# Sliding-window attention in a one-core layer kernel: transposing the probabilities in 32 by 32 blocks on VectorE and placing them by on-chip DMAs

## The chip, the cores and the metric

The kernel runs on one core of a Trainium2 chip. A core has engines that work at the same time, each through its own queue, in order: TensorE (PE, with its weight loads PEld), VectorE (DVE), ScalarE (ACT), GpSimd (POOL), and SyncE (SP), which here issues most DMAs; 16 DMA engines move the data. The metric is the device time of one execution in microseconds, lower being better.

## What is computed

One layer on x of 2048 tokens by 1024: token mixing, cross-attention to 256 memory tokens, and a SwiGLU feed-forward, each between RMS norms. Token mixing projects the normed x to 2816 columns: 512 for the queries of a sliding attention (8 heads of 64), 128 for its keys and 128 for its values (2 heads of 64, each for four query heads), and four times 512 for a gated recurrence (HGRN2). The change is in the sliding attention alone:

```python
def swa_with_sinks(q, k, v, sinks):
    # a token of chunk c (64 tokens) reads every token of chunks c-2 .. c
    s = jnp.einsum('bnqhgd,bnkhd->bnhgqk', qc, kband) * (Dh ** -0.5)
    s = jnp.where(valid, s, NEG_INF)
    p = jax.nn.softmax(jnp.concatenate([s, sink], axis=-1), axis=-1)[..., :L]
    return jnp.einsum('bnhgqk,bnkhd->bnqhgd', p, vband)
```

## The kernel before

All is computed in float32 precision. The matmuls of projections and sliding attention run on float32r operands, and an operand is split into a high part (a rounded copy) and a low part (the rest), so that a product is two or three matmuls (`mm3`, L151: high x high, high x low, low x high).

The program has stages. First `in_first` (L466) norms x and projects the first 1024 tokens, writing the columns to `z_d` in device memory, and then key and value columns of the second 1024 tokens. From about 264 to 605 us three things are traced side by side in `mix` (L216 to L237): sliding attention, one position n of 128 tokens at a time (16 of them); the first eight positions of the recurrence; and `in_proj`, which projects the second 1024 tokens, one block of 128 columns at a time, 48 matmuls of 512 columns each (L156 to L158). Then the rest of the recurrence with the folding of the cross-attention's weights, and from about 760 us the output projection, cross-attention and feed-forward as large products (L1162 to L1164).

The program is written as generators that take turns, but what stands in each engine's queue is decided by a scheduler, which orders the instructions by its own timeline. Once built, each queue is fixed and runs in order, and an instruction that waits holds all behind it on its engine.

A position of sliding attention is in two halves. `swa_front` (L773) loads queries and keys twice, once to partitions 0 to 63 and once to 64 to 127, and splits them on the way: the queries by ScalarE and VectorE (L787, L788), the keys by GpSimd and VectorE (L798). Because high and low parts of the queries stand on the two halves of the partitions, two matmuls do for the scores (L822, L823). VectorE takes mask and maximum (L827), ScalarE the exponentials with their sums (L831), GpSimd and VectorE finish the sink and the reciprocal (L834 to L839), and VectorE scales (L842). `swa_back` (L845) is called one position later. TensorE transposes the probabilities, four blocks of 128 by 128 into one PSUM bank (L856); ScalarE writes their high part (L860), VectorE the low part (L861); TensorE multiplies with the values (L865, L866), whose high and low parts are beside each other, so that the result comes as two halves on the partitions, which are added (L869, L870) and stored to `y_d`. The tiles of this pool have one buffer where no number is given: `kr`, `kl`, `kh`, `ys`; `S` has six, which is three per pair of heads of two positions.

Of the kernel before, what the change touches and what calls it, by code (L numbers as in the profile page):

```python
# [48 lines left out]
class Layer:  # L49
# [111 lines left out]
    def run(self):  # L161
# [4 lines left out]
        self.z_d = tc.dram_tile([DIN, T], F32, name="z_d")  # L166

# [298 lines left out]
    def in_first(self):  # L466
# [154 lines left out]
        z = self.pair_tile()  # L621
        for s in range(2):
            for i in range(2):
# [3 lines left out]
                nc.scalar.activation(z[:, i, s * 512:(s + 1) * 512], ps, AF.Copy)  # L627
        for i in range(2):
            self.store(self.z_d[c0 + i * P:c0 + (i + 1) * P, TB:2 * TB], z[:, i, :])
        return u  # L630

    def in_block(self, ca, cb, x, ahead, beside, get, plain, between):
# [16 lines left out]
        def out(i, j, a, b):  # L649
            c0 = (ca, cb)[i] * P  # L650
            if plain:
                self._n += 1
                t = self.st_pool.tile([P, 512], F32, tag="part", name=f"zp_{self._n}", bufs=3)
                nc.scalar.activation(t, a, AF.Copy)
                self.store(self.z_d[c0:c0 + P, j * 512:(j + 1) * 512], t)
                return
            if not z:
                z.append(self.pair_tile())
            zs = z[0][:, i, j * 512:(j + 1) * 512]
# [16 lines left out]
        def after():  # L676
# [14 lines left out]
            for i, c in enumerate(() if plain else (ca, cb)):  # L691
# [17 lines left out]
    def in_cols(self, b, u, cols, e1):  # L709
# [5 lines left out]
        for s in range(TB // 512):  # L715
            sl = slice(s * 512, (s + 1) * 512)
            for i, c in enumerate(cols):
# [4 lines left out]
                if c0 < C_QH or C_IH <= c0 < C_GH:  # L722
# [11 lines left out]
        for i, c in enumerate(cols):  # L734
# [5 lines left out]
            self.store(self.z_d[c0:c0 + P, b * TB:(b + 1) * TB], z[i])  # L740
# [32 lines left out]
    def swa_front(self, n, kinds):  # L773
# [7 lines left out]
        for g in range(2):  # L781
            qd = ph.tile([P, 4, P], F32, tag="qd", name=f"qd{n}_{g}", bufs=2)
            qsrc = z[g * 256:(g + 1) * 256, t0:t0 + P].rearrange("(h d) t -> d h t", d=64)
            self.load(qd[0:64], qsrc)
            self.load(qd[64:128], qsrc)
            q = ph.tile([P, 4, P], F32R, tag="qs", name=f"qs{n}_{g}", bufs=2)
            nc.scalar.activation(q, qd, AF.Copy, scale=-0.125)  # L787
            nc.vector.scalar_tensor_tensor(q[64:128], qd[64:128], -0.125, f32(q[64:128]), ALU.mult, ALU.subtract)  # L788
            qs.append(q)

        kr = ph.tile([P, 2, M], F32, tag="kr", name=f"kr{n}")
        kl = ph.tile([P, 2, M], F32R, tag="kl", name=f"kl{n}")
        kh = ph.tile([P, 2, M], F32R, tag="kh", name=f"kh{n}")
# [1033 lines left out]
```

## Time and profile before

| | us |
|---|---|
| median of three runs (2533.18, 2534.37, 2536.8) | 2534.37 |
| span of the profiled execution, first to last instruction | 2530.8 |
| stage of sliding attention (264 to 605): VectorE on 62 low parts (L861) | 42.3 |
| the same: ScalarE on 62 high parts (L860) | 36.8 |

The profile is of one execution on the chip, and of it the span is given. A row of a group of instructions gives line, engine, operation, what is written and read, shapes and count, then busy time in us, mean duration in ns, and the engine's idle time before them with what ended it. A row by windows gives for each engine the busy time and the count, then the granted TensorE clock (1.00 is full), the share of the DMA engines, and GB/s. A row of the timeline begins with start and duration. TensorE's matmuls overlap, so one's duration is longer than the time it takes from the queue.

### The profile page before, as it was taken

Reading aid. Unit: us, or ns where it says so; the run is one execution under the profiler, and the core shown is the slowest. Engines: PE = TensorE matmul, PEld = TensorE weight load, DVE = VectorE, ACT = ScalarE, POOL = GpSimd, SP = SyncE. Lnnn points to the kernel's source line nnn. Section 1 sums busy time; section 2 is a strip of 40 time slices with the busy share of each in tenths; the row PEclk is TensorE's granted clock in tenths of the full one; section 3 lists DMA queues with packets and bytes.
Section 4 is the critical chain, followed back from the end, with each engine's and each line's share of the span. In section 5 each row is a group of like instructions: output and inputs, shape, how many; then the busy total and the mean of one; then the engine's idle time right before and its main releaser. Section 6 shows DMA issues by size and latency. Waiting matters only on the chain.

```text
span 2530.8 us, 34134 instructions
## 1 busy us (share of the span) xinstructions
PE 2496.8 (99%) x11942; PEld 2087.0 (82%) x11942; DVE 1794.5 (71%) x2863; ACT 1262.1 (50%) x2627; POOL 375.2 (15%) x540
## 2 busy tenths in 40 slices
PE   9999999999999999999999999999999999999998
PEld 8878888888987888878878888888888888888886
DVE  8785488986557889988866655576566557664766
ACT  5453466655565576566753333353333335443543
POOL 4231344321401111112200000000000000000022
PEclk9999999999999999999999999999999999999999
DMA  6455645673887996758944322254354334565776
GB/s 199 152 167 177 176 145 156 199 248 114 276 311 261 299 335 196 251 175 256 346 161 168 135 77 93 80 192 154 129 208 167 117 130 155 182 178 112 228 173 153
DMA packets 305133, 470.07 MB, mean 186 GB/s; under 512 B 21440, under 2 KB 193472, under 8 KB 304960
## 3 DMA queue, kind: packets, MB, share of 16 engines
q1 hardware_dynamic: 298912, 445.86, 52.7%
q0 software_dynamic: 6048, 22.02, 5.1%
q8 instruction: 94, 1.54, 0.3%
q14 instruction: 79, 0.65, 0.1%
HBM read 301.09 MB, written 166.72 MB: 185 GB/s over the span
## 4 chain that ended last, share of the span: by engine, by line
PE 84%; DVE 6%; DMA 4%; ACT 3%; issue 2%; POOL 1%; SPq 0%; DVEq 0%; POOLq 0%; ACTq 0%
PE psm L1164 23%; PE psm L1162 23%; PE psm L1163 22%; PE psg L156 2%; PE psg L158 2%; PE psg L157 2%; DVE T L1002 1%; DVE S L1002 1%; DMA raw<-in_wo_x_dram 1%; ACT junk L1533 1%; SPq L75 0%; DMA row<-h_d 0%; PE pss L156 0%; PE pss L157 0%; PE pss L158 0%
## 5 line engine op out<-in xcount | busy, mean ns | idle before, releaser
L1162 PE MATMUL psm<-T,S 128*128 128x512 f32 x2680 | 1034.3, 391 | 10.3 <-ACT part L1177 5.6
L1163 PE MATMUL psm<-T,S 128*128 128x512 f32 x2680 | 1042.9, 390 | 1.5 <-DVE T L1002 1.4
L1164 PE MATMUL psm<-T,S 128*128 128x512 f32 x2680 | 1029.8, 390 | 3.7 <-DVE S L1002 3.7
L1162 PEld LDWEIGHTS psm<-T,S 128*128 128x128 f32 x2680 | 503.2, 188 | 122.5 <-ACT part L1177 9.9
L1164 PEld LDWEIGHTS psm<-T,S 128*128 128x128 f32 x2680 | 503.4, 188 | 111.1 <-DVE S L1002 6.7
L1163 PEld LDWEIGHTS psm<-T,S 128*128 128x128 f32 x2680 | 503.5, 188 | 107.2 <-DVE T L1002 3.7
L999 ACT ACTIVATE S<-sum 128x512 fp32r<-128x512 f32 (+1 forms) x370 | 224.3, 620 | 375.7 <-PE psm L1164 274.2
L1002 DVE TENSOR_TENSOR S<-sraw,S 128x512 fp32r<-128x512 f32 (+1 forms) x315 | 212.1, 680 | 237.2 <-ACT S L999 234.1
L1177 ACT ACTIVATE part<-psm 128x512 f32<-128x512 f32 x285 | 168.8, 597 | 260.4 <-PE psm L1164 241.9
L1002 DVE TENSOR_TENSOR S<-sum,S 128x512 fp32r<-128x512 f32 (+1 forms) x388 | 258.5, 675 | 45.2 <-ACT S L999 41.2
L999 ACT ACTIVATE S<-sraw 128x512 fp32r<-128x512 f32 (+1 forms) x300 | 184.4, 618 | 109.2 <-PE psm L1164 107.3
L1566 POOL DMA_DIRECT2D y_d<-row x16 | 14.1, 879 | 1077.0 <-DVE row L1748 1026.1
L1002 DVE TENSOR_TENSOR T<-row,T 128x1024 fp32r<-128x1024 f32 (+1 forms) x112 | 131.0, 1186 | 27.7 <-ACT T L999 25.7
L156 PE MATMUL psg<-u,whi 128*128 128x512 f32 x320 | 127.6, 399 | 1.3 <-DVE z L730 1.3
L158 PE MATMUL psg<-u,wlo 128*128 128x512 f32 x320 | 127.4, 399 | 0.0
L157 PE MATMUL psg<-u,whi 128*128 128x512 f32 x320 | 127.4, 398 | 0.0
L1533 ACT ACTIVATE junk<-row 128x512 f32<-128x512 f32 x160 | 99.7, 625 | 43.5 <-DVE row L1555 21.2
L999 ACT ACTIVATE T<-row 128x1024 fp32r<-128x1024 f32 (+1 forms) x112 | 113.4, 1032 | 7.3 <-DMA row<-in_w_down_dram 2.8
L1699 DVE TENSOR_TENSOR row<-psm,part 128x512 f32<-128x512 f32 x66 | 44.1, 688 | 71.3 <-PE psm L1164 71.3
L1002 DVE TENSOR_TENSOR wlo<-raw,whi 128x1024 fp32r<-128x1024 f32 x52 | 64.0, 1232 | 41.4 <-ACT whi L999 30.6
L1748 DVE TENSOR_TENSOR row<-psm,part 128x512 f32<-128x512 f32 x72 | 49.2, 689 | 49.3 <-PE psm L1164 49.1
L831 ACT ACTIVATE S<-S,w_mn 128x256 f32<-128x256 f32 (+1 forms) x128 | 63.1, 496 | 41.4 <-DVE w_mn L827 41.0
(355 smaller groups left out, 3541.3 us busy)
## 6 DMA issues: line engine op xcount, KB each, us to landing
sraw<-in_w_gate_dram SPq DMA_DIRECT2D x44, 512.0 KB, 3.8
sraw<-in_w_up_dram SPq DMA_DIRECT2D x44, 512.0 KB, 3.7
hid_d<-row SPq DMA_DIRECT2D x44, 512.0 KB, 2.7
sraw<-hid_d SPq DMA_DIRECT2D x32, 512.0 KB, 4.4
sraw<-in_w_in_dram SPq DMA_DIRECT2D x48, 256.0 KB, 3.8
z_d<-pair SPq DMA_DIRECT2D x20, 512.0 KB, 3.3
raw<-in_w_in_dram SPq DMA_DIRECT2D x20, 512.0 KB, 4.6
z_d<-z SPq DMA_DIRECT2D x20, 512.0 KB, 3.8
```

The source lines that it names most:

```text
L156: nc.tensor.matmul(ps, ah, bh, start=(i == 0), stop=False)
L157: nc.tensor.matmul(ps, ah, bl, start=False, stop=False)
L158: nc.tensor.matmul(ps, al, bh, start=False, stop=(i == n - 1))
L831: nc.scalar.activation(s[:, r, o:], s[:, r, o:], AF.Exp, bias=mn[:, i:i + 1], scale=-1.0, accum_out=den[:, i:i + 1])
L999: self.nc.scalar.activation(hi, raw, AF.Copy)
L1002: self.nc.vector.tensor_tensor(lo, raw, f32(hi), ALU.subtract)
L1162: nc.tensor.matmul(ps, s[:, 0, k, :], t[:, 0, k, :], start=st, stop=False, **kw)
L1163: nc.tensor.matmul(ps, s[:, 0, k, :], t[:, 1, k, :], start=False, stop=False, **kw)
L1164: nc.tensor.matmul(ps, s[:, 1, k, :], t[:, 0, k, :], start=False, stop=sp, **kw)
L1177: nc.scalar.activation(t, ps, AF.Copy)
L1533: self.nc.scalar.activation(junk, a, AF.Square, scale=float(D) ** -0.5, accum_out=to)
L1748: nc.vector.tensor_tensor(d, a, b, ALU.add)
```

## The change

Four things are changed together.

1. *Splits where made.* Query and key columns are no longer written to `z_d`. `halved_store` writes a scaled high part (ScalarE) and a low part (VectorE) and stores both, in `zq_d` and `zk_d`. It is called in `in_first`, `in_block` and `in_cols`. `swa_front` loads the halves as they are, queries into four `qs` buffers and keys into one `kk`.
2. *Transposition.* `swa_turn` is new. Four VectorE transposes turn the 32 by 32 blocks of a position's probabilities into `pb`; 16 DMAs from buffer to buffer, each with 32 partitions and 64 KB, place the blocks in `pt`. Both have one buffer. It is called after `swa_back` of the position before.
3. `swa_back` makes the high part by ScalarE, and the low part by VectorE in place in `pt`, 1024 columns a time.
4. The two halves of the result are added by the store: one DMA writes the first half to `y_d`, and one that GpSimd issues accumulates the second. `S` has four buffers in place of six.

```diff
+    def halved_store(self, c0, t0, src, hi, lo):
+        nc = self.nc
+        dst, r, f = (self.zq_d, c0, -0.125) if c0 < C_KA else (self.zk_d, c0 - C_KA, 1.0)
+        n = hi.shape[1]
+        nc.scalar.activation(hi.bitcast(F32R), src, AF.Copy, scale=f)
+        nc.vector.scalar_tensor_tensor(lo.bitcast(F32R), src, f, hi, ALU.mult, ALU.subtract)
+        for e, t in enumerate((hi, lo)):
+            self.store(dst[e, r:r + P, t0:t0 + n], t)
...
-            qd = ph.tile([P, 4, P], F32, tag="qd", name=f"qd{n}_{g}", bufs=2)
-            self.load(qd[0:64], qsrc)
-            self.load(qd[64:128], qsrc)
-            q = ph.tile([P, 4, P], F32R, tag="qs", name=f"qs{n}_{g}", bufs=2)
-            nc.scalar.activation(q, qd, AF.Copy, scale=-0.125)
-            nc.vector.scalar_tensor_tensor(q[64:128], qd[64:128], -0.125, f32(q[64:128]), ALU.mult, ALU.subtract)
+            q = ph.tile([P, 4, P], F32R, tag="qs", name=f"qs{n}_{g}", bufs=4)
+            for e in range(2):
+                self.load(f32(q[64 * e:64 * e + 64]),
+                          self.zq_d[e, g * 256:(g + 1) * 256, t0:t0 + P].rearrange("(h d) t -> d h t", d=64))
...
-        self.split(kr[:, :, o:], kh[:, :, o:], kl[:, :, o:])
+        kk = ph.tile([P, 2, 2, M], F32R, tag="kk", name=f"kk{n}", bufs=1)
...
-                s = ph.tile([P, 2, M], F32, tag="S", name=f"S{n}_{g}{i2}", bufs=6)
+                s = ph.tile([P, 2, M], F32, tag="S", name=f"S{n}_{g}{i2}", bufs=4)
...
+    def swa_turn(self, n, S, nk):
+        nc, ph = self.nc, self.sw
+        o = M - nk * P
+        t = ph.tile([P, 2, 2, 4, P], F32, tag="pb", name=f"pb{n}")
+        for g in range(2):
+            to = t[:, g, 2 - nk:].rearrange("p k b (h j) -> p (k b) h j", h=4)
+            for i2 in range(2):
+                nc.vector.transpose(to[:, :, 2 * i2:2 * i2 + 2],
+                                    S[2 * g + i2][:, :, o:].rearrange("p r (b i) -> p b r i", i=32))
+        d = ph.tile([P, 2, 2, 4, P], F32R, tag="pt", name=f"pt{n}")
+        for a in range(4):
+            for b in range(4):
+                self.load(f32(d[b * 32:(b + 1) * 32, :, 2 - nk:, a, :]), t[a * 32:(a + 1) * 32, :, 2 - nk:, b, :])
+        return d
...
-                for i in range(4):
-                    nc.tensor.transpose(ps[:, i * P:(i + 1) * P],
-                                        S[2 * g + i // 2][:, i % 2, o + kb * P:o + (kb + 1) * P], self.ident)
-                nc.scalar.activation(th, ps, AF.Copy)
-                nc.vector.tensor_tensor(tl, ps, f32(th), ALU.subtract)
+            lo = pt[:, g, 2 - nk:].rearrange("p k a c -> p k (a c)")
+            hi = ph.tile([P, 2, 512], F32R, tag="pth", name=f"pth{n}_{g}", bufs=2)[:, 2 - nk:]
+            nc.scalar.activation(hi, f32(lo), AF.Copy)
+            nc.vector.tensor_tensor(lo, f32(lo), f32(hi), ALU.subtract)
...
-            nc.scalar.activation(ys[a], pr[c], AF.Copy)
-            nc.vector.tensor_tensor(ys[a], pr[a], ys[a], ALU.add)
-        self.store(self.y_d[n, :, 0:512], ys.rearrange("p k t -> p (k t)"))
+            nc.scalar.activation(ys[:, g, :].rearrange("p (h a j) -> p a h j", h=4, a=4),
+                                 ps.rearrange("p (a h j) -> p a h j", h=4, a=4), AF.Copy)
+        dst = self.y_d[n, :, 0:512].rearrange("(g d) c -> d g c", g=2)
+        self.store(dst, ys[0:64])
+        nc.gpsimd.dma_start(dst, ys[64:128], accum_op=ALU.add)
...
+                last = n, kinds(n), self.swa_turn(n, S, len(vs)), vs
```

The change also moves instructions in the queues. Line numbers in the rows of the changed kernel are its own.

TensorE, late in sliding attention. Before, in the products of position 13 (L865 high part, L866 low part), there are projection matmuls (L156 to L158 on `psg`) and the transposes (L856):

```order
L157 MATMUL psg_6424<-u_10_2207,whi_6419 128x512
L158 MATMUL psg_6424<-u_10_2207,wlo_6420 128x512
L156 MATMUL psg_6424<-u_10_2207,whi_6419 128x512
L157 MATMUL psg_6424<-u_10_2207,whi_6419 128x512
L158 MATMUL psg_6424<-u_10_2207,wlo_6420 128x512
L856 MATMUL pss_6063<-ident,S_10_5794 128x128 x2
L856 MATMUL pss_6063<-ident,S_11_5804 128x128 x2
L856 MATMUL pst_6072<-ident,S_10_5794 128x128 x2
L856 MATMUL pst_6072<-ident,S_11_5804 128x128
L866 MATMUL psh_6056<-ptl_00_6044,vst_5542 128x512
```

Now, from position 11 (`pth_1_5475` and `pt_5299`; L901 high part, L902 low part) to the end, scores (L850, L851; `kk_5577` is of position 13) and products follow each other:

```order
L901 MATMUL pst_5475<-pth_1_5472,vst_5011 128x512
L850 MATMUL pst_5590<-kk_5577,qs_0_5571 128x256
L851 MATMUL pst_5590<-kk_5577,qs_0_5571 128x256
L850 MATMUL pst_5590<-kk_5577,qs_0_5571 128x256
L851 MATMUL pst_5590<-kk_5577,qs_0_5571 128x256
L902 MATMUL pss_5466<-pt_5299,vst_5011 128x512
L901 MATMUL pss_5466<-pth_0_5463,vst_5204 128x512
L902 MATMUL pss_5466<-pt_5299,vst_5204 128x512
L902 MATMUL pst_5475<-pt_5299,vst_5011 128x512
L901 MATMUL pst_5475<-pth_1_5472,vst_5204 128x512
L902 MATMUL pst_5475<-pt_5299,vst_5204 128x512
L850 MATMUL pst_5633<-kk_5577,qs_1_5574 128x256
```

Transposes and projection matmuls are gone from between the products; from the first product of position 10 to the last of position 15 only three projection matmuls stand in the queue, all among the products of position 10.

SP, in the same part of the program, each row with the semaphores that it waits for; DMAHW0 to DMAHW7 are those of SP's own DMAs, used in turn. Before (queries `qd`, keys `kr`, weights and stores):

```order
L75 DMA qd_0_5519<-z_d 64x4x128 [waits DMAHW6_49,DVE_49]
L75 DMA qd_0_5519<-z_d 64x4x128 [waits DMAHW7_49]
L75 DMA qd_1_5525<-z_d 64x4x128 [waits DMAHW0_49,DVE_49]
L75 DMA qd_1_5525<-z_d 64x4x128 [waits DMAHW1_49]
L78 DMA out_s<-u_5091 128x1024 [waits DMAHW2_49,DVE_49]
L75 DMA kr_5531<-z_d 64x2x256 [waits DMAHW3_49,Pool_49]
L75 DMA kr_5531<-z_d 64x2x256 [waits DMAHW4_49]
L75 DMA x_5729<-in_w_out_dram 128x1024 [waits DMAHW5_49]
```

Now, the transfers of position 12 from `pb` to `pt`, the first 12 rows of 17:

```order
L75 DMA pt_5488<-pb_5483 32x4x128 [waits DMAHW1_49,DVE_49,PE_49]
L75 DMA pt_5488<-pb_5483 32x4x128 [waits DMAHW2_49]
L75 DMA pt_5488<-pb_5483 32x4x128 [waits DMAHW3_49]
L78 DMA y_d<-ys_5462 64x2x512 [waits DMAHW4_49,Activation_49]
L75 DMA pt_5488<-pb_5483 32x4x128 [waits DMAHW5_49]
L75 DMA pt_5488<-pb_5483 32x4x128 [waits DMAHW6_49]
L75 DMA pt_5488<-pb_5483 32x4x128 [waits DMAHW7_49]
L75 DMA pt_5488<-pb_5483 32x4x128 [waits DMAHW0_49]
L75 DMA pt_5488<-pb_5483 32x4x128 [waits DMAHW1_49]
L75 DMA pt_5488<-pb_5483 32x4x128 [waits DMAHW2_49]
L75 DMA pt_5488<-pb_5483 32x4x128 [waits DMAHW3_49]
L75 DMA pt_5488<-pb_5483 32x4x128 [waits DMAHW4_49]
```

Sixteen transfers are added to SP's queue for each position, with the store of the result of the position before as fourth among them; the first waits for VectorE and TensorE, and each for the DMA eight places earlier.

VectorE, late in sliding attention. Before, low parts from PSUM (L861) stand among projection work and the scaling (L842):

```order
L861 TENSOR_TENSOR ptl_00_6044<-pss_6038,pth_00_6043 128x512
L861 TENSOR_TENSOR ptl_01_6053<-pst_6047,pth_01_6052 128x512
L1002 TENSOR_TENSOR wlo_6529<-raw_6526,whi_6528 128x1024
L730 SCALAR_TENSOR_TENSOR z_6305<-z_6305,psg_6333 128x512
L839 RECIPROCAL w_rd_5998<-w_dn_5996 128x4
L839 RECIPROCAL w_rd_6031<-w_dn_6029 128x4
L842 TENSOR_SCALAR S_00_5973<-S_00_5973,w_rd_5998 128x256 x2
```

Now, block transposes of position 12 (`pb_5483`, L881), then low parts of position 11 (`pt_5299`, L898), then the maximum of position 13 (L855):

```order
L870 TENSOR_SCALAR S_11_5441<-S_11_5441,w_rd_5456 128x256 x2
L881 STREAM_TRANSPOSE pb_5483<-S_00_5398 128x8x64
L881 STREAM_TRANSPOSE pb_5483<-S_01_5408 128x8x64
L881 STREAM_TRANSPOSE pb_5483<-S_10_5431 128x8x64
L881 STREAM_TRANSPOSE pb_5483<-S_11_5441 128x8x64
L898 TENSOR_TENSOR pt_5299<-pt_5299,pth_0_5463 128x1024
L898 TENSOR_TENSOR pt_5299<-pt_5299,pth_1_5472 128x1024
L855 ISA S_00_5589,w_mn_5587<-pst_5590,wmask,nsink 128x256
```

The transposes of a position have come ahead of the low parts of the position before it.

More of the change, by code (lines that the diff above doesn't have):

```diff
@@ L690, in after @@
                                                    e[:, 0, sl], ALU.mult, ALU.mult)
[L691 removed]
+            for i, c in enumerate(() if plain or c0 < C_VA else (ca, cb)):
                 self.store(self.z_d[c * P:(c + 1) * P, 0:TB], z[0][:, i, :])
@@ L739, in in_cols @@
                     pass
-            self.store(self.z_d[c0:c0 + P, b * TB:(b + 1) * TB], z[i])
+            if c0 >= C_VA:
+                self.store(self.z_d[c0:c0 + P, b * TB:(b + 1) * TB], z[i])
         return e1
```

81 lines of the change are left out of this document (46 added, 35 removed).

## Prediction

> **What bounds the kernel now.** I read the page's totals and chain first, then the stage in which sliding attention runs (264 to 605 us) by windows, then TensorE's own rows there.
>
> ```profile
> span 2530.8 us, 34134 instructions
> ...
> PE 2496.8 (99%) x11942; PEld 2087.0 (82%) x11942; DVE 1794.5 (71%) x2863; ACT 1262.1 (50%) x2627; POOL 375.2 (15%) x540
> ...
> PE 84%; DVE 6%; DMA 4%; ACT 3%; issue 2%; POOL 1%; SPq 0%; DVEq 0%; POOLq 0%; ACTq 0%
> ```
>
> ```profile
> 264.00:585.00 321.00, 317.94 (x1778) 273.51 (x1777) 267.65 (x651) 196.82 (x576) 114.04 (x172) 0.99 0.57 184
> 585.00:605.00 20.00, 18.28 (x103) 14.95 (x101) 16.03 (x45) 13.29 (x37) 1.45 (x5) 0.91 0.28 92
> ```
>
> TensorE is busy 317.94 of 321 us in the stage, VectorE 267.65, ScalarE 196.82, the DMA engines 0.57: TensorE is the bound almost to the end of the stage, and only the last 20 us have a gap worth naming. So matmuls taken out of the stage shorten it by their slots on TensorE, as long as something else stands ready to fill the queue. TensorE works in order, and a busy time holds overlapping matmuls, so a slot is read from start to start:
>
> ```profile
> 295.97 0.28 PE L822 MATMUL pss<-kh,qs 128*128 128x256 f32 x1
> 296.09 0.28 PE L823 MATMUL pss<-kl,qs 128*128 128x256 f32 x1
> 296.21 0.40 PE L156 MATMUL psg<-u,whi 128*128 128x512 f32 x1
> 296.44 0.39 PE L157 MATMUL psg<-u,whi 128*128 128x512 f32 x1
> 296.67 0.60 PE L856 MATMUL pss<-ident,S 128*128 128x128 f32 x4
> 297.02 0.48 PE L158 MATMUL psg<-u,wlo 128*128 128x512 f32 x1
> 297.34 0.39 PE L156 MATMUL psg<-u,whi 128*128 128x512 f32 x1
> ```
>
> A score matmul takes 0.12 us (295.97 to 296.09), a 512-wide one 0.23 (296.21 to 296.44), four transposes 0.35 (296.67 to 297.02) and 0.09 more on the matmul behind them (0.32 for 0.23): 0.44 us.
>
> **The change, part by part.**
>
> ```profile
> L856 PE MATMUL pst<-ident,S 128*128 128x128 f32 x120 | 21.5, 277 | 0.2 <-DVE w_mn L827 0.2
> L856 PE MATMUL pss<-ident,S 128*128 128x128 f32 x128 | 21.5, 277 | 0.8 <-DVE w_mn L827 0.8
> ```
>
> *Removed on TensorE.* 120 + 128 = 248 transposes are 62 groups of four: 62 x 0.44 = **27.3 us**, all on the bound. Nothing is added there: the order has 248 matmuls fewer, and score and value products keep their number and width.
>
> *VectorE and ScalarE.*
>
> ```profile
> L1002 DVE TENSOR_TENSOR T<-row,T 128x1024 fp32r<-128x1024 f32 x105 | 126.4, 1219 | 27.4 <-ACT T L999 25.3 <-DMA row<-u_s 1.7
> L999 ACT ACTIVATE T<-row 128x1024 fp32r<-128x1024 f32 x105 | 109.3, 1058 | 6.9 <-DMA row<-d_s 2.8 <-DMA row<-in_w_down_dram 2.4 <-DMA row<-qk_s 0.7
> ...
> L1431 DVE STREAM_TRANSPOSE row<-row 128x512 f32<-128x512 f32 x64 | 40.6, 684 | 0.0
> ...
> L788 DVE SCALAR_TENSOR_TENSOR qs<-qd,qs 64x512 fp32r<-64x512 f32 x32 | 25.8, 809 | 21.1 <-ACT qs L787 20.2
> ...
> L861 DVE TENSOR_TENSOR ptl<-pss,pth 128x512 fp32r<-128x512 f32 x32 | 21.9, 684 | 0.3 <-ACT pth L860 0.2
> ...
> L861 DVE TENSOR_TENSOR ptl<-pst,pth 128x512 fp32r<-128x512 f32 x30 | 20.4, 679 | 1.5 <-PE pss L866 1.5
> ```
>
> VectorE gains 64 block transposes (64 x 0.684 = 44 us) and 32 subtractions of 1024 columns (32 x 1.22 = 39), and loses the 62 of 512 (21.9 + 20.4 = 42) and the query split (25.8); with the key split and the last add gone too, the sum is about level or some 10 us less. The splits moved to where queries and keys are made add 20 operations of about 0.7 us, 14 us, most of them in the stage before 264 us, beside a busy TensorE. I cost these at nothing while TensorE's queue is full, with 2 us for the head of the kernel, where only three buffers take two halves a block; uncovered they cost up to 14.
>
> The rule that speaks against the change begins with rows: four 128 by 128 transposes hold TensorE for 0.44 us, while one VectorE transpose of the same 512 columns lasts 0.684 and leaves blocks that 16 transfers must still place. The Trainium skill, "VectorE: DVE Perf Modes", section "Rules for kernel authors", says to transpose 128 by 128 on TensorE where a PSUM destination will do, and VectorE only within a 32 by 32 bank. It gives no time for the placing, so the sum below stands on rows alone.
>
> *The path that is new.* Before, the probabilities went from TensorE through PSUM to ScalarE and VectorE. Now one position's link is: block transposes on VectorE, 16 DMAs on SP, the high part on ScalarE, the low part on VectorE, the products. `pb` and `pt` have one buffer each. So the transposes of n+1 wait for the DMAs of n to have landed, and the DMAs of n+1 wait for the products of n, which read `pt`. That is a loop, and its period C bounds the positions from below. Its DMAs are bounded by these rows:
>
> ```profile
> h1t_d<-row SPq DMA_DIRECT2D x64, 128.0 KB, 4.5
> ...
> un_d<-pair SPq DMA_DIRECT2D x32, 128.0 KB, 2.3
> ...
> y_d<-ys SPq DMA_DIRECT2D x16, 256.0 KB, 3.9
> ...
> vr<-z_d SPq DMA_DIRECT2D x16, 64.0 KB, 3.1
> ```
>
> ```profile
> 126.66 1.84 SPq L78 DMA_DIRECT2D un_d<-pair  x4
> ```
>
> The order shows that each DMA of SP waits for the one eight places earlier, so at most eight are under way. Sixteen and the store of `ys` among them are 17, three rounds of one landing each. No row shows a DMA from buffer to buffer. Nearest is vr, of the same 64 KB and in this stage: 3 x 3.1 = 9.3 us. The quick end is un_d (3 x 2.3 = 6.9; issuing 16 at 1.84/4 = 0.46 comes to 7.4 without the last landing, so it is no shorter), the slow end h1t_d, from a stage of heavy traffic: 13.5.
>
> The Trainium skill, "DMA: Bandwidth & Descriptors", section "Anatomy of one DMA", gives a fixed 2.0 us or so and bytes over 436 GB/s: an estimate of 2.15 us for 64 KB, 6.5 for three rounds, and 14 us less in the sum below. The trace's landings of 2.3 to 4.5 us lie above it.
>
> C, then, for a late position: four transposes 2.5 us (40.6/64 = 0.63 each back to back; they come first on VectorE), two low parts 2.4, the three matmuls that must wait for the second 3 x 0.23 and the last one's end, 1.2, an allowance of 0.4 for handoffs, the three rounds 9.3, and 0.7 in which the store of `ys`, fourth in the row of DMAs, waits for ScalarE's copy and holds those behind it on SP. Sum: **16.5 us**, ends 13 and 21. The high parts (1.06 us) lie beside the transposes.
>
> *Where C shows.* In the order, positions up to n = 10 have input-projection matmuls between them: 75 between the last product of n = 9 and the first of n = 10, so 17 us at 0.23. The link from product to product is the three rounds, the `ys` wait and a high part, 11 to 12 us, so these positions stay on TensorE's time; I put 3 us for waits in them. But the filler runs out: from the first product of n = 10 to the last of n = 15 only three projection matmuls stand in TensorE's queue, all at n = 10. Each of these five periods holds 16 score and 8 value matmuls, 16 x 0.12 + 8 x 0.23 = 3.8 us. So TensorE has 19 us of work in 5 x 16.5 = 82.5 us and **stands idle for 63.5**. In the order before, projections stand between the products up to the last two positions. Their waits go:
>
> ```profile
> 591.42 0.63 PE L856 MATMUL pss<-ident,S 128*128 128x128 f32 x4
> 592.85 0.51 PE L865 MATMUL psh<-pth,vst 128*128 128x512 f32 x1 [0.80 <-DVE ys L870]
> 594.12 0.65 PE L856 MATMUL pss<-ident,S 128*128 128x128 f32 x4 [0.77 <-DVE w_mn L827]
> ```
>
> ```profile
> 590.00:598.00 8.00, 6.28 (x32) 4.59 (x31) 7.90 (x28) 6.52 (x22) 0.83 (x4) 0.85 0.49 164
> ```
>
> From 591.42 to 592.85 there is 1.0 us over the transposes' 0.44, to 594.12 another 1.0 over 0.23, and a granted clock of 0.85 over 8 us costs 1.2: **3 us** that the new gap replaces. The same row shows the clock falling after a gap, so the products on the loop may run at half speed in the long gaps; that is inside C's bounds.
>
> *Also added.* POOL issues 16 accumulating DMAs and loses 15 key splits.
>
> ```profile
> L1566 POOL DMA_DIRECT2D y_d<-row x16 | 14.1, 879 | 1077.0 <-DVE row L1748 1026.1 <-ACT row L1752 44.5 <-DMA row<-d_s 6.4
> ```
>
> Each takes POOL 0.88 us and waits there for the store of `ys` to land (3.9 us), and behind it on POOL stands the sum of the softmax of n+2, for which its scaling and its transposes wait. Products done after 6.5 us, copy 0.6, landing 3.9, issue 0.9 and some 2 for the scaling make 14 of the period's 16.5, so it is covered; with quick DMAs it is what holds C up. SP's 256 further issues, at 0.46 us 118 us of a stage of 341, delay weights that are fetched ahead.
>
> *Sum*, on the profiled execution: 2530.8 - 27.3 - 3 + 63.5 + 3 + 2 = 2569. Its span is 3.6 us under the median of the runs, 2534.4, to which I add the same 38: **2572**.
>
> **The rivals.**
>
> *The removed slots win: faster.* If the blocks land fast and links overlap, the gap shrinks below what is removed. Without the 5 us of small waits the balance is at 5C - 19 = 30.3, so C = 9.9; the loop as I add it has a quick end of 13. At C = 7 the time is 2534.4 - 30.3 + 16 = 2520. For it: no row shows such a DMA. Against it: the transposes, low parts and products alone take 6.1 of the 9.9. Chance 0.07.
>
> *They balance*, C near 10: 2534. Chance 0.05.
>
> *The loop is late with filler as well.* VectorE has 83% of the stage, SP's transfers pass among 512 KB ones, and at three rounds of 4.5 us the link is 16 us, the length of its filler: any wait at VectorE then shows at each of some nine positions. With C = 21 the gap is 5 x 21 - 19 = 86, and 2 us at nine positions make 18: 2534.4 - 30.3 + 86 + 18 + 2 = 2610. For it: h1t_d's landing. Against it: the DMA share of 0.57 there, and vr's 3.1. Chance 0.18.
>
> **How the numbers follow.** My forecast has 0.70, at C from 13 to 20: 5 x 13 - 19 = 46 gives 2534.4 - 30.3 + 46 = 2550 without small waits, C = 20 gives 2534.4 - 30.3 + 81 + 5 = 2590. The range goes to 2543 on the quick side and takes in half of the last rival, to 2604; left out are the first two cases and its upper part, about 0.2. A difference under 0.2%, 5 us, is about what a measurement of this kernel can't tell from none. Faster 0.07, same 0.05, slower 0.88.
>
> **What would show it.** In the profile after: no L856 group; TensorE full to about 20 us earlier than now, then five gaps of some 12 us, each ended by the high or low part; a granted clock near 0.5 there; SP's bursts of 16 lasting 7 to 10 us. I am wrong if TensorE's gaps after the filler sum to under 30 us, if a burst lands within 4 us, or if the gaps stand at the positions with filler.

## The result, and the profile after

The changed kernel takes 2638.8 us, median of four runs (2637.9 to 2639.5), against 2535.6 before in the same comparison: 1.0404 times, 95% interval 1.0391 to 1.0417, slower by 103 us. The forecast was 2572, range 2543 to 2604: the sign was right, the size was not. First the page of the profile after (totals, and the chain):

```profile
span 2637.7 us, 33856 instructions
...
PE 2498.0 (95%) x11694; PEld 2079.0 (79%) x11694; DVE 1784.9 (68%) x2821; ACT 1239.5 (47%) x2552; POOL 366.3 (14%) x540
...
PE 73%; DMA 9%; DVE 7%; SPq 5%; ACT 3%; issue 3%; POOL 1%; DVEq 0%; ACTq 0%; POOLq 0%
```

248 matmuls are gone, as said, yet TensorE's busy time is unchanged (2496.8 before): part of what remains runs at a lower clock. The chain now goes through transfers (9% for 4%) and SP's queue (5% for 0%). By windows, of the head of the kernel before, then of three stretches after:

```profile
60.00:200.00 140.00, 136.61 (x599) 111.77 (x599) 114.75 (x154) 72.00 (x113) 45.40 (x56) 1.00 0.54 167
```

```profile
60.00:200.00 140.00, 128.10 (x533) 102.66 (x532) 113.41 (x152) 69.67 (x109) 38.04 (x55) 0.95 0.50 157
...
264.00:560.00 296.00, 279.99 (x1443) 237.31 (x1443) 200.30 (x464) 138.66 (x404) 102.92 (x147) 0.98 0.87 230
...
600.00:705.00 105.00, 27.55 (x97) 21.11 (x98) 44.89 (x128) 32.70 (x93) 8.01 (x20) 0.60 0.55 127
```

At the head 66 matmuls fewer fit into the same 140 us, 15.2 us at 0.23. From 600 to 705 us TensorE is busy 27.55 of 105 us, at a granted clock of 0.60: the gap that was forecast, but longer. The middle row has gaps too, which the forecast put at 3 us; the same stretch before:

```profile
264.00:560.00 296.00, 292.94 (x1646) 252.51 (x1645) 242.98 (x585) 179.73 (x527) 108.55 (x161) 0.99 0.57 183
```

TensorE's idle time there grew from 3 to 16 us. That is one of the prediction's own signs of being wrong, gaps at the positions with filler. Who waits for what in the stage (264 to 720 us), by groups:

```profile
L881 DVE STREAM_TRANSPOSE pb<-S 128x512 f32<-128x512 f32 (+1 forms) x64 | 39.3, 665 | 38.6 <-DMA pt<-pb 37.3 <-issue 1.2
...
L897 ACT ACTIVATE pth<-pt 128x1024 fp32r<-128x1024 f32 (+1 forms) x32 | 31.2, 1023 | 86.6 <-DMA pt<-pb 86.0 <-issue 0.6
...
L901 PE MATMUL pss<-pth,vst 128*128 128x512 f32 x31 | 16.4, 529 | 78.4 <-ACT pth L897 78.4
```

TensorE waits 78.4 us for the high part, and ScalarE, before it, 86 for the transfers. One period late in the stage, rows of the timeline by engine (the products of position 12 end at 646.71 + 0.63, those of 13 at 668.83 + 0.39):

```profile
646.71 0.63 PE L902 MATMUL pst<-pt,vst 128*128 128x512 f32 x1
...
661.51 0.79 PE L901 MATMUL pss<-pth,vst 128*128 128x512 f32 x1 [12.87 <-ACT pth L897]
...
663.84 0.55 PE L850 MATMUL psh<-kk,qs 128*128 128x256 f32 x1 [1.32 <-DMA kk<-zk_d]
...
666.97 0.63 PE L902 MATMUL pss<-pt,vst 128*128 128x512 f32 x1
...
667.40 0.63 PE L901 MATMUL pss<-pth,vst 128*128 128x512 f32 x1
...
668.83 0.39 PE L902 MATMUL pst<-pt,vst 128*128 128x512 f32 x1
```

```profile
647.37 1.94 SPq L75 DMA_DIRECT2D pt<-pb  x3
649.40 0.62 SPq L78 DMA_DIRECT2D y_d<-ys  x1
650.07 8.78 SPq L75 DMA_DIRECT2D pt<-pb  x13
658.95 1.28 SPq L75 DMA_DIRECT2D kk<-zk_d  x2
```

```profile
660.42 2.49 DVE L881 STREAM_TRANSPOSE pb<-S 128x512 f32<-128x512 f32 x4 [4.77 <-DMA pt<-pb]
662.84 2.32 DVE L898 TENSOR_TENSOR pt<-pt,pth 128x1024 fp32r<-128x1024 f32 x2
```

The first transfer is issued 0.03 us after the last product: that is the loop through `pt`. Then SP issues without a pause, 13 in 8.78 us, **0.675 us each**, until 658.85; the high part starts at 660.40, 1.5 us after the last issue. Burst and landing are 13.0 us, the rest of the loop 8.8: a period of 21.9 us where 16.5 were forecast (the last five are 26.9, 22.0, 21.9, 20.1 and 20.0). In the rest stand scores that wait for keys, which SP issued only behind the burst, and products 0.43 us apart (666.97 to 667.40) in place of 0.23.

The burst is not made of rounds of landings. The median landing of these transfers, and SP's own waits for them in the whole stage (us in total, times, longest):

```profile
pt<-pb SPq DMA_DIRECT2D x240, 64.0 KB, 2.3
```

```profile
SPq L75 <- DMA pt<-pb: 1.4, 1, 1.4
```

A transfer has landed 2.3 us after its issue, three to four issues later. So the DMA eight places earlier, for which each must wait, had nearly always landed: SP waited once.

The profile of before held this price, but also lower ones. Loads of queries, of the recurrence, and of values:

```profile
498.15 2.68 SPq L75 DMA_DIRECT2D qd<-z_d  x4
```

```profile
307.07 0.38 SPq L75 DMA_DIRECT2D qq<-z_d  x1
...
310.65 0.33 SPq L75 DMA_DIRECT2D vr<-z_d  x1
```

Four loads in 2.68 us are 0.67 us each. The prediction took 0.46 from `un_d`. All four, like the new transfers, move runs of 128 numbers, so the length of the runs doesn't tell which price will hold; what does is not shown.

### The profile page after: what moved, and what is told of

Same layout as the page of the kernel before. It is cut to its first block, busy times and chain, and to the rows that moved or that the text cites. A ratio compares the mean times of both kernels' runs of the same rounds, so it can differ in the third digit from the quotient of the medians.

```text
span 2637.7 us, 33856 instructions
## 1 busy us (share of the span) xinstructions
PE 2498.0 (95%) x11694; PEld 2079.0 (79%) x11694; DVE 1784.9 (68%) x2821; ACT 1239.5 (47%) x2552; POOL 366.3 (14%) x540
## 4 chain that ended last, share of the span: by engine, by line
PE 73%; DMA 9%; DVE 7%; SPq 5%; ACT 3%; issue 3%; POOL 1%; DVEq 0%; ACTq 0%; POOLq 0%
PE psm L1202 21%; PE psm L1200 21%; PE psm L1201 21%; SPq L75 4%; DVE T L1040 1%; DMA x<-in_w_out_dram 1%; DVE S L1040 1%; DMA qs<-zq_d 1%; PE psg L156 1%; PE psg L158 1%; PE psg L157 1%; DMA row<-d_s 1%; DMA kk<-zk_d 1%; DMA raw<-in_wo_x_dram 1%; DMA pair<-in_x_dram 1%
## 5 line engine op out<-in xcount | busy, mean ns | idle before, releaser
L1200 PE MATMUL psm<-T,S 128*128 128x512 f32 x2680 | 1035.5, 391 | 15.2 <-ACT part L1215 7.0
L156 PE MATMUL psg<-u,whi 128*128 128x512 f32 x320 | 128.7, 402 | 0.0
L158 PE MATMUL psg<-u,wlo 128*128 128x512 f32 x320 | 127.8, 400 | 0.0
L1737 DVE TENSOR_TENSOR row<-psm,part 128x512 f32<-128x512 f32 x66 | 44.0, 687 | 71.3 <-PE psm L1202 71.3
L901 PE MATMUL pss<-pth,vst 128*128 128x512 f32 x31 | 16.4, 529 | 78.4 <-ACT pth L897 78.4
```

What stands on the lines that cost most here:

```text
L156: nc.tensor.matmul(ps, ah, bh, start=(i == 0), stop=False)
L158: nc.tensor.matmul(ps, al, bh, start=False, stop=(i == n - 1))
L1200: nc.tensor.matmul(ps, s[:, 0, k, :], t[:, 0, k, :], start=st, stop=False, **kw)
```

## The experiments

The table gives each kernel's time, its ratio to the kernel before (95% interval), and when in its trace the products of positions 0, 7, 8 and 15 ended, in us. The last column is the end of the stage. Each ratio is to the runs of the kernel before that were taken beside it; their medians lie between 2533.8 and 2535.6. By these intervals only e8_part can't be told from before.

| | us | ratio | 0 | 7 | 8 | 15 |
|---|---|---|---|---|---|---|
| before | 2535.6 | | 310.5 | 471.6 | 492.6 | 604.3 |
| changed | 2638.8 | 1.0391-1.0417 | 326.9 | 509.8 | 541.1 | 709.3 |
| e1_splits | 2543.2 | 1.0021-1.0048 | 325.2 | 480.1 | 498.7 | 612.0 |
| e2_turn | 2608.7 | 1.0277-1.0312 | 308.1 | 485.6 | 527.0 | 678.2 |
| e3_two | 2634.8 | 1.0380-1.0411 | 324.3 | 499.8 | 546.9 | 706.9 |
| e4_queues | 2623.8 | 1.0338-1.0369 | 322.9 | 494.1 | 538.5 | 695.0 |
| e5_one | 2569.1 | 1.0109-1.0139 | 318.3 | 461.4 | 531.8 | 641.5 |
| e6_quarter | 2625.4 | 1.0331-1.0365 | 323.3 | 496.0 | 539.2 | 695.8 |
| e7_half | 2566.8 | 1.0103-1.0137 | 306.1 | 464.0 | 518.3 | 633.3 |
| e8_part | 2535.5 | 0.9992-1.0011 | 319.5 | 474.3 | 492.9 | 606.3 |
| e9_kk | 2645.0 | 1.0421-1.0450 | 323.8 | 509.2 | 550.8 | 716.9 |
| e10_all | 2567.2 | 1.0113-1.0141 | 315.5 | 454.6 | 525.7 | 637.3 |
| e14_kk | 2630.6 | 1.0367-1.0398 | 323.7 | 502.1 | 543.4 | 702.8 |
| e15_pt | 2609.0 | 1.0281-1.0311 | 324.0 | 489.6 | 547.8 | 683.1 |
| e16_hop | 2615.5 | 1.0306-1.0340 | 319.4 | 490.4 | 541.9 | 685.5 |
| e17_hopz | 2609.9 | 1.0284-1.0315 | 305.0 | 478.7 | 551.3 | 679.8 |
| e18_bank | 2548.8 | 1.0034-1.0068 | 321.4 | 464.2 | 490.5 | 622.5 |
| e20_best | 2600.1 | 1.0244-1.0278 | 316.0 | 481.5 | 514.0 | 673.2 |

**Is the burst as long as its issuing, or as its bytes?** Same bytes with one issue:

```diff
-        for a in range(4):
-            for b in range(4):
-                self.load(f32(d[b * 32:(b + 1) * 32, :, 2 - nk:, a, :]), t[a * 32:(a + 1) * 32, :, 2 - nk:, b, :])
+        self.load(f32(d[:, :, 2 - nk:]), t[:, :, 2 - nk:])
```

> The changed kernel with one transfer of 1 MB from pb to pt in place of the sixteen of 64 KB: the same bytes, one issue. The blocks are not put in their places, so the attention's output isn't the reference's. Theory: all sixteen positions, with projection matmuls or without, stand on one loop (end of the products, burst of sixteen, halves, products), and the burst is the time that SP takes to issue it; with one issue burst and landing are some 6.5 us in place of 13, periods fall by as much, and the stage comes near TensorE's own work: 2530 to 2560, with the transposes' 27 us partly showing. Rival: the burst lasts as long as its bytes need; one transfer of 1 MB lands after 11 us or more, and the time stays above 2610.

2569.1 us, 9 above the upper end of the forecast: 70 of the 103 us are gone. Position 14's transfer, on SP, and the high part behind it, on ScalarE:

```profile
618.64 0.52 SPq L75 DMA_DIRECT2D pt<-pb  x1
```

```profile
623.49 2.00 ACT L895 ACTIVATE pth<-pt 128x1024 fp32r<-128x1024 f32 x2 [0.60 <-DMA pt<-pb]
```

1 MB is there 4.85 us after its issue began (the median landing in this run is 6.0), where sixteen pieces took 13.0. Same issues with a quarter of the bytes (and one `pt` tile for all positions):

```diff
-                self.load(f32(d[b * 32:(b + 1) * 32, :, 2 - nk:, a, :]), t[a * 32:(a + 1) * 32, :, 2 - nk:, b, :])
+                self.load(f32(d[b * 32:(b + 1) * 32, :, 2 - nk:, a, 0:32]), t[a * 32:(a + 1) * 32, :, 2 - nk:, b, 0:32])
```

> The changed kernel with the sixteen transfers cut to a quarter of their bytes (32 of the 128 columns of each): the same issues, a quarter of the bytes, in one pt tile that lives through the stage. Three quarters of the probabilities are left out of the products' right place, so the output isn't the reference's. Theory: issuing is as long as before, the burst stays at 11 us and the time within 15 us of the changed kernel's 2639. Rival: the bytes decide; the burst falls under 8 us and the time under 2590.

2625.4 us, and the burst is no shorter:

```profile
615.12 1.94 SPq L75 DMA_DIRECT2D pt<-pb  x3
617.16 0.62 SPq L78 DMA_DIRECT2D y_d<-ys  x1
617.82 8.55 SPq L75 DMA_DIRECT2D pt<-pb  x13
```

0.66 us each for 16 KB, 0.675 for 64 KB. By themselves the two runs don't tell issuing from rounds of landings, since one transfer is one round and sixteen small ones are as many as before. But the small ones land in 2.0 us (median):

```profile
pt<-pb SPq DMA_DIRECT2D x240, 16.0 KB, 2.0
```

Three rounds of that would be 6 us, and issuing them took 11.25. With SP's track and waits above, that leaves issuing. The Trainium skill, "Perfetto Trace Analysis", section "What 'DMA-bound' means", describes this picture: an issuing engine's track solid with DMA slices is bound by generating descriptors, not by moving data. The trace agrees. Half of the sixteen from ScalarE's queue:

```diff
+                q = nc.scalar if a % 2 else nc.sync
+                q.dma_start(f32(d[b * 32:(b + 1) * 32, :, 2 - nk:, a, :]), t[a * 32:(a + 1) * 32, :, 2 - nk:, b, :])
```

> The changed kernel with half of the sixteen transfers of each position issued by ScalarE in place of SP. Theory: a burst of sixteen is as long as its issuing, 11.5 us, so two queues make it about 6, the period falls from 22 to 16.5, and SP's queue, full between 264 and 560 us, brings queries, keys and weights earlier: some 28 us less in the tail and some 10 in the filled stretch, about 2600. Rival: the burst is as long as the transfers themselves take (eight under way at a time, or 1 MB through the DMA engines): it stays near 11 us and the time near 2639.

2623.8, 15 less and not 39. The last burst, on SP and on ScalarE's queue, and the high part:

```profile
678.32 1.23 SPq L887 DMA_DIRECT2D pt<-pb  x2
679.60 0.62 SPq L78 DMA_DIRECT2D y_d<-ys  x1
680.27 4.55 SPq L887 DMA_DIRECT2D pt<-pb  x6
```

```profile
678.33 6.03 ACTq L887 DMA_DIRECT2D pt<-pb  x8
...
688.25 2.00 ACT L898 ACTIVATE pth<-pt 128x1024 fp32r<-128x1024 f32 x2 [9.33 <-DMA pt<-pb]
```

Issuing took 6.5 us as expected, but the high part came 3.4 us after the last issue, not 1.5: 9.9 for 13.0. So the transfers themselves come next, and the rival holds in part; whether by their bytes or by something else on their way is not shown.

**The head.** The kernel before with part 1 of the change alone (the diff of `halved_store` and of the loads, above):

> The kernel before with only the first part of the change: queries and keys split where they are made and loaded as halves; transposes on TensorE, products and store as before. Theory: the gaps at the head of the changed kernel (60 to 200 us, some 15 us more of them than before) come from the splits at making, which stand in ScalarE's and VectorE's queues and hold buffers until SP has stored them; then this kernel is slower than before by about 15 us, 2550, with its gaps between 60 and 200 us, and level after 264 us. Rival: those gaps belong to the whole change as the scheduler orders it, and the splits are hidden; then 2537 or less, no gaps at the head.

```profile
60.00:200.00 140.00, 128.32 (x545) 103.37 (x544) 114.46 (x153) 71.18 (x111) 39.95 (x55) 0.98 0.52 160
```

At the head (the row is 60 to 200 us) 545 matmuls for 599, 12 us, of which 3 come back later: 2543.2, 9 us slower, where 15 were expected. Then the same with more buffers (six in this stage):

```diff
-                    t.append(self.st_pool.tile([P, 512], F32, tag="part", name=f"zp_{self._n}", bufs=3))
+                    t.append(self.st_pool.tile([P, 512], F32, tag="part", name=f"zp_{self._n}", bufs=self.parts))
```

> Splits where made alone, as in the first run, with six buffers in place of three for the tiles in which the first stage writes its halves (part). Theory: the gaps at the head come from buffers that are held until SP has stored both halves; with six they go back from 17 to some 7 us between 60 and 200 us, and the time falls to about 2533. Rival: they come from the two operations themselves in ScalarE's and VectorE's queues; then nothing changes, 2543.

```profile
60.00:200.00 140.00, 131.70 (x570) 107.33 (x569) 117.89 (x159) 71.81 (x114) 46.12 (x56) 0.99 0.53 166
```

2535.5, level with before, though 29 matmuls are still missing at the head. Buffers it was, for about half of the gaps: 570 matmuls now. One more `pair` tile (`bufs=6`), with five `part`, was meant to take the rest:

> Splits where made alone, with five part buffers and six pair buffers. Theory: the gap of 4.8 us at 109 us that is left with six part buffers comes from pair tiles, of which a block of queries now takes two; with one more the head is as before, and the 5 us that the lighter sliding stage gains show: 2530. Rival: that gap is the order of ScalarE's and VectorE's queues there: 2535.

It gave 2541.3 (1.0017 to 1.0035): the time gives no sign that the rest is that buffer, but as `part` went from six to five as well, the run can't rule it out. The other way round, parts 2 to 4 of the change without part 1:

> The changed kernel without its first part: queries and keys are loaded and split as before, the rest (block transposes, transfers, 1024-wide halves, accumulating store) as changed. Theory: the head is as before, so 15 us less than the changed kernel, and the sliding stage keeps its long periods: 2623, with the last five periods still near 22 us. Rival: the new query and key loads, which wait in SP's queue behind the transfers, are what makes the stage late, and loads with splits make it later still or free it: 2639 or more, or below 2610 with periods under 19 us.

```profile
60.00:200.00 140.00, 136.34 (x597) 111.58 (x596) 114.31 (x154) 71.74 (x113) 45.47 (x56) 1.00 0.53 166
```

2608.7: 30 us less than the whole change, 14 under the forecast. The head accounts for about half (597 matmuls), and the products of position 0 end 19 us earlier. The periods from there are 370 us long in place of 382, the last three 19.2, 20.3 and 19.8, below the 22 of the forecast but not under 19; which load or split makes these 12 is not settled.

**What is on the loop.** Two `pt` buffers, paid for with one `pth` and three `qs`:

```diff
-        d = ph.tile([P, 2, 2, 4, P], F32R, tag="pt", name=f"pt{n}")
+        d = ph.tile([P, 2, 2, 4, P], F32R, tag="pt", name=f"pt{n}", bufs=2)
```

> The changed kernel with two buffers for pt (one pth and three qs buffers pay for it). Theory: the loop is held by SP's issuing, 0.68 us for each of 17, and closed through pt; with two buffers the first transfer of a position no longer waits for the products of the one before, and what is left is issuing, landing and the block transposes, 10.8 + 1.6 + 2.5 and some 0.7, so periods of 15.5 to 16 us in place of 22, five of them: 30 us less, 2609. Rival: the wait through pt is not what ends last (the scores' keys, ScalarE's and VectorE's halves are), and the periods stay above 20 us: 2630 to 2640.

2634.8, inside the rival's range. But with one `pth` the second high part waits for the first products, so this run says nothing on `pt`. Again with three `pth` of 512 columns (`hi` made in two pieces), `ys` added by VectorE as before, and three `qs`:

> The changed kernel with two buffers for pt and three pth buffers of 512 columns (the earlier run with two pt had a single pth, which held the second half back); ys as before the change and three qs buffers pay for it. Theory: products are no longer on the loop, which is then block transposes 2.5, issuing 11.5, landing 1.6, that is 15.6 us; the late periods fall from 22 to 16 to 17 and the time to 2600 or less. Rival: SP's queue, with all loads behind the bursts, keeps positions at 20 us or more: 2625 to 2640.

2609.0, 30 us less than the change; the last three periods are 17.0, 14.8 and 16.3 us. So the products do stand on the loop. Without them the periods are near the 15.6 us reckoned for the loop through `pb`: block transposes, issuing and landing. The total missed the forecast by 9, and `ys` and `qs` changed with `pt`, so the 30 us are not its own alone. Keys ahead of the burst (`kk` with `bufs=2`), first with three `qs`:

> The changed kernel with two buffers for the keys kk (three for qs, to make room), so that SP has a position's keys ahead of the burst of sixteen in its queue and not behind it. Theory: in the late periods of 22 us the scores wait about 2 us for keys that SP issued only after the burst, and the products stand behind the scores in TensorE's queue; without that, periods near 20 us and fewer such waits in the filled stretch: 2620 to 2628. Rival: ScalarE's and VectorE's halves end last anyway: 2635 to 2640.

2645.0: the last three periods fell to 19.1, 19.6 and 18.7, but the products of position 8 ended 10 us later than in the changed kernel. With four `qs` and the old `ys`:

> The changed kernel with two buffers for the keys, all four for the queries; room comes from ys, whose two halves are added by VectorE as before the change, in place of the accumulating store. Theory: the run with two kk and three qs buffers gained 2 us in each of the last periods and lost it to queries that came late; with four the gain stays, and the time is 2620 to 2628. Rival: keys behind the burst cost nothing on the whole, the queue of SP decides: 2635 or more.

2630.6, 8 us less than the change, 3 above the forecast: late keys are at most a minor part. The old `ys` may have part in the 8, and that three `qs` were what cost e9_kk its gain is likely, not shown.

**Half of the heads.** The kernel before, with only heads 4 to 7 turned (`swa_turn` for `g == 1` and `n < 14`, two `pt` of half the size):

> The kernel before, with the probabilities of only the second four heads turned by VectorE and sixteen transfers of 32 KB, in positions 0 to 13, and two pt buffers; the first four heads, positions 14 and 15, the loads, splits and the store as before. 108 transposes go, 27 slots of 0.44, 12 us. Theory (a loop whose period must be shorter than TensorE's work of a position, some 21 us): with two buffers only issuing and landing, 12 us, and the block transposes, 1.3, are on it, so it hides: 2525. Rival: SP's sixteen issues for each position hold back loads, or the period is bound by the products all the same: 2540 to 2560.

2566.8, slower by 31, above what the rival had. Its transfers are half as large but as many, sixteen for each position, and between the products of positions 11 and 14 its order has no projections.

**What is left when issuing is cheap.** One transfer, two `kk` (and, as in e9_kk, three `qs`), six `part`:

> The changed kernel with one transfer of 1 MB in place of sixteen (blocks not in their places, so the attention's output isn't the reference's), two kk buffers, and six part buffers at the head. Theory: the three prices add: 2569 less 8 (head) less 5 to 15 (keys), 2546 to 2556; still slower than before, because block transposes, one landing, halves and products remain in series in the late positions while the projections that could fill TensorE are used up earlier. Rival: with these three gone TensorE alone binds, and the 27 us of transposes show: 2515 or less.

2567.2: the prices don't add, though the three `qs` may have cost here what they seem to cost in e9_kk. With this bank order positions 0 to 7 are early in the quick versions, and the products of position 8 end at 518 to 551 whatever the link costs; in e5_one 216 projection matmuls stand between those of 7 and 8, and none after position 11. Position 8 is the first whose scores go to a third PSUM tag, which the recurrence uses:

```diff
-                swa = self.swa(range(NT), lambda n: "st" if n < NPB else "sth")
+                swa = self.swa(range(NT), lambda n: "st")
```

> One misplaced transfer of 1 MB in place of sixteen, as in the earlier run (the attention's output isn't the reference's), and positions 8 to 15 use the same two PSUM tags (s, t) as the first eight, not a third (h) that the recurrence holds to its end near 500 us. Theory: what was left of the slowdown there, 34 us, is that position 8 stands behind the recurrence for that bank, so that the first positions run ahead and use up projections (216 of their matmuls stand between the products of positions 7 and 8) and the last five find none; with other banks the order has projections up to position 13, TensorE binds again and part of the transposes' 27 us shows: 2520 to 2545. Rival: the chain of a position, with one landing, is too long by itself: 2560 or more.

```profile
60.00:200.00 140.00, 124.87 (x518) 99.69 (x517) 111.88 (x151) 69.48 (x108) 40.13 (x54) 0.95 0.50 156
```

2548.8: of the 34 us that e5_one had left, 20 are gone. The step from 7 to 8 is 26.3 us in place of 70.4. (The kernel before wasn't run with two tags; its step is 21.0.) The time is still 15 above before, between the two forecasts: the head (518 matmuls for 599, 19 us) takes most of what the transposes gave, and the last two periods, 13.7 and 12.4, find no projections.

**Blocks placed with fewer issues.** Four writes to device memory and one read:

```diff
+            for a in range(4):
+                self.load(w[:, :, a, g, 2 - nk:].rearrange("p b g k c -> p b (g k c)"),
+                          t[a * 32:(a + 1) * 32, :, g, 2 - nk:].rearrange("p b g k c -> p b (g k c)"))
...
+            self.load(f32(d[:, :, g, 2 - nk:]).rearrange("p a g k c -> p a (g k c)"),
```

> The changed kernel with another way of placing: four transfers of 256 KB from pb to device memory, each writing 2 KB runs, and one of 1 MB back to pt, five issues for sixteen; the result is the same. Theory: five issues, 2.5 us, and two landings of about 3 and 4.5 are 10 us in place of 13.1; one transfer in place of sixteen took 8.2 us from this link and 70 from the time, 8.5 for each, so 26 less: 2612. Rival: two landings one after the other, with 3 MB moved for each position, are no shorter than sixteen issues: 2635 or more.

2615.5, near the 2612 of the forecast, but by luck: the two landings (medians) are longer than I took, and the link is not 10 us.

```profile
pb_d<-pb SPq DMA_DIRECT2D x60, 256.0 KB, 5.4
...
pt<-pb_d SPq DMA_DIRECT2D x15, 1024.0 KB, 7.9
```

Late in the stage, from SP and from ScalarE:

```profile
599.32 2.91 SPq L75 DMA_DIRECT2D pb_d<-pb  x4
...
609.35 0.93 SPq L75 DMA_DIRECT2D pt<-pb_d  x1
610.95 1.92 SPq L75 DMA_DIRECT2D pb_d<-pb  x4
```

```profile
619.20 2.00 ACT L904 ACTIVATE pth<-pt 128x1024 fp32r<-128x1024 f32 x2 [12.75 <-DMA pt<-pb_d]
```

From 599.32 to 619.20 the link takes 19.9 us; the last five links take 12 to 20. But the writes of the next position start at 610.95, before the products of this one (they end at 625.5): only the read back waits for `pt`. That overlap is the likely gain; no run tests it alone.

> The same placing through device memory, in the kernel without splits where made (queries and keys loaded and split as before). Theory: the two gains add, 2609 less 26 is 2583, still slower than before, since the link of about 18 us in the late positions has no projections left beside it. Rival: with SP's queue short and the head as before, the stage is TensorE's again: 2535 or less.

2609.9, 27 above the forecast: the gains of e2_turn and e16_hop don't add, for the reason above (position 7 ends at 479, position 8 at 551). Last, what helped, together:

> The correct placing by sixteen transfers with what helped: two pt buffers and three pth (ys as before the change, three qs), six part buffers at the head, and the two PSUM tags for all positions. Theory: 2609 less 8 for the head and less 15 to 30 for the bank is 2571 to 2586; still slower than before, since SP's issuing keeps late periods at 16 us and nothing stands beside them. Rival: with filler beside its late positions TensorE binds: 2540 or less, or, if the bank was not what held position 8, 2600.

2600.1: of the versions that place all blocks the best, and 2.6% slower than before. No version with block transposes, not even those that misplace the blocks, was as fast as the kernel before. One run more, e8_part with the accumulating store and the values split by one copy and one subtraction, without the turn (the values' copy is a part of the change that the list of four doesn't name):

> Splits where made with six part buffers, and two more pieces of the change, without its transposes: values split by one copy and one subtraction, and the halves of the result added by the store. Theory: TensorE binds the stage, so lighter ScalarE and VectorE queues change only the last two positions: 2532 to 2535. Rival: the accumulating store, which waits for the first store on GpSimd, holds the softmax sums behind it and delays late positions: 2540 or more.

2539.8 (1.0012 to 1.0030), 4 us above e8_part, between the two forecasts: these pieces bring nothing, and whether the store on GpSimd costs the 4 isn't shown.

## Why the prediction was wrong

Right: the 248 slots are gone; projections stop at position 10; the last five positions stand on a loop through `pb` and `pt` with TensorE at a low clock (0.60, forecast near 0.5); the direction. Of the terms of the sum three were too small, the first of them by a wrong mechanism.

- **C, the step that failed.** "Three rounds of one landing each", 9.3, and 0.7 for `ys`, made 10.0. Measured, at position 13: issuing 11.5 and 1.5 of landing, 13.0. A landing was even shorter than the 3.1 us assumed, 2.3, so three rounds of it would be 6.9. What made the burst long is the count of issues at 0.675 us, and SP hardly ever waited for the DMA eight places earlier. I had weighed issuing and dismissed it with 0.46 us, a row of another transfer. The rest, 6.5, measured 8.8: keys behind the burst, and products at about half speed. The last five periods, from 598.4 to 709.3, are 110.9 us with 19 of work at full speed, which leaves **91.9 where 63.5 were forecast**. Not all of it is idle: TensorE is busy 33.1 us in these periods, since the same work lasts longer at a clock of 0.60:

```profile
598.40:709.00 110.60, 33.13 (x119) 25.81 (x119) 47.01 (x130) 34.44 (x98) 8.81 (x22) 0.60 0.54 128
```

- **Positions with filler.** I put 3 us for waits. The stage ends 105 us later, although 27.3 us of transposes are gone; 15.2 us of work came over from the head. So the time that TensorE doesn't work at full speed grew by 105 + 27.3 - 15.2 = 117.1; less the 88.9 by which it grew in the tail (91.9 for 3), **28.2** lie before position 10's products end. The link was not the 11 to 12 us that I set against 17 us of filler: burst and landing alone are 13. And filler used while waiting is gone at the end.
- **The head.** 2 us for 15.2. I had named both the three buffers and the price when uncovered, up to 14, and taken the cover for granted. That 14 is so near is luck: it prices VectorE's operations, and e8_part puts about half of the gaps down to the buffers.
- After the stage another 1.9.

2530.8 - 27.3 + 15.2 + 117.1 + 1.9 = 2637.7, the span. This closes by construction, since the 117.1 come from the end of the stage; what it gives is the shares of the miss: of 68.7 us over the forecast for the span, 28.4 in the tail, 25.2 with filler, 13.2 at the head, 1.9 after. The rival "late with filler as well", at C = 21 (2610), came nearest, with 18 us for waits and 2 for the head. Its period was right by luck, as it took three rounds of 4.5 us. The rule that I weighed against the change, TensorE for 128 by 128 transposes (the Trainium skill, "VectorE: DVE Perf Modes", section "Rules for kernel authors"), holds here: 27 us of slots stand against sixteen issues for each position. The estimate of 2.15 us for a landing (the Trainium skill, "DMA: Bandwidth & Descriptors", section "Anatomy of one DMA") is from a fit for DMAs that GpSimd issues; SP issues these, and their median is 2.3.

Open: what makes an issue take 0.67 us and not 0.33; the 12 us of e2_turn's periods; the other half of the gaps at the head; how much of the 28.2 is issuing and how much position 8's bank; and why e20_best stayed 14 us above its forecast.

## What to carry to other kernels

Price a burst of small transfers both ways, by landings in rounds and by issuing, count times an issue time from the rows, and take the longer. Where rows of like transfers differ (0.33 to 0.67 us here), the highest belongs into the range. When a serial chain is lengthened, multiply by all its positions: other work that hides the early ones is not there for the late ones. Where a stage starts to write two tiles for one, look for the buffer count before calling the work hidden.

## What was not expected of the hardware

- SP's issue time hung on the count of transfers and not on bytes: 0.66 us for 16 KB, 0.675 for 64 KB in the same pattern, and 0.52 for one of 1 MB.
- A buffer to buffer transfer of 1 MB was in place 4.85 us after its issue began, in a quiet stretch; sixteen of 64 KB from two queues landed 3.4 us after the last issue, from one 1.5. The Trainium skill, "DMA: Bandwidth & Descriptors", section "Issuing engines are not separate DMA queues", says that more issuing engines save only the time to issue, usually small beside the transfer. For one transfer that holds here too, 0.675 of 2.3 us. But for sixteen in a row issuing was the larger part, 11.5 of 13.0 us, and two queues brought 15 us.
